# Two row-wise projections back to back, and another place for the fetched rows' products on VectorE, in a hybrid decoder block

## The chip, the cores and the metric

The kernel runs on one core of one Trainium2 chip. The metric is the device time of one execution in microseconds (us). The engines that matter here are TensorE (PE in the rows, PEld its weight loads), VectorE (DVE), ScalarE (ACT), GpSimd (POOL) and SyncE (SP), which issues the plain DMAs.

## What is computed

One decoder block over 256 tokens of width 2048 in float32: a norm, a projection whose columns feed two attentions and two gates, an output projection, and then a mixer in which each token picks 128 of 16384 experts. Cut to what matters:

```python
h = rms_norm(x, g_mix)
z = h @ w_in
q_a, k_a, v_a, c_q, c_kv, k_r, gate_a, gate_b = split(z)      # c_q: 512 columns, c_kv + k_r: 320
...
q = rms_norm(c_q, g_cq) @ w_uq                                # MLA: latent rows, normed again
kv = rms_norm(c_kv, g_ckv) @ w_ukv
...
x = x + mixed @ w_o
# PEER: u, v are (16384, 2048); expert (tokens, 128) holds indices, gate their weights
a = einsum('cd,ced->ce', h2, u[expert])
w = gelu(a) * gate
x = x + einsum('ce,ced->cd', w, v[expert])
return rms_norm(x, g_final)
```

## The kernel before

Every weight comes as a float32 tile `raw` and is split in two parts, `whi` (rounded to TensorE's fp32r format, on ScalarE, L108) and `wlo` (the remainder, on VectorE, L112). Three matmuls per product then give float32 accuracy: high by high, low by high, high by low. `feed_hi` loads and splits one unit of weights; there are three buffers for `raw` and two each for `whi` and `wlo`, so that a unit's `whi` can only be written when TensorE has read the unit two before it.

**The front.** `nblock` (L159) multiplies rows of tokens by streamed weights. The first projection, `pss_cq` (512 columns, 16 steps of six matmuls), runs while x is still being loaded; `make_x` scales x by the norm's gain for it, called from `ahead_x`. The norm's own factor does not go into the matmuls: `r1c` (one number a token) is applied to the finished rows by `rows_out` (L338), and `r1` (the same, laid along the free axis) to transposed results. To get it, ScalarE squares the rows of x (L248, eight instructions), VectorE sums them, ScalarE takes a root (L171), VectorE finishes the reciprocal root (L172 to L176) and makes two diagonal tiles `dg` (L255), and TensorE multiplies ones by them (L256). In the code this whole chain stands between `pss_cq` and the second row-wise projection, `rows_proj(320, ckr)` (L376). Then come the norms of the two latents (`norm_rows`), their transposes through TensorE (`tp`, L386 to L391), a rotary part `kro` that needs `sin` and `cos`, and the projection of kT (L146 and L151).

Up to the experts a scheduler sets each engine's order from the code; from L945 on the order is that of the code.

**The first expert sweep** (L948 to L1007) has 128 units. In unit j TensorE multiplies 16 high tiles (L952) and then 16 low tiles (L981) of `u` by the tokens' transposes, for 192 of the 256 tokens; in some units eight small matmuls (L958) that build a gate grid `G` stand between. VectorE multiplies earlier results (L962), adds two halves of the last unit's result (`add`, L905), and subtracts to make `wlo` of unit j+1 (`ready_lo`, L977); products with a finished grid follow (L979), and a comparison for a later grid (L940).

The other 64 tokens' experts are fetched row by row. `gathered()` is a generator with 130 steps: a step asks GpSimd for the next indirect DMA of 128 rows (L828) into one of two `urow` buffers and multiplies the previous one on VectorE by the tokens (L852, which also sums). The request for row i+1 writes the buffer that product i-1 has read, so GpSimd waits for that product. `gather_to(goal)` advances it; 54 steps (GU) belong to this sweep, spread evenly from the unit JR on (52 here), the rest to the second sweep (L1036), which multiplies by `v`.

Of the kernel before, what the change touches and what calls it, by code (L numbers as in the profile page):

```python
# [8 lines left out]
F32 = mybir.dt.float32  # L9
# [3 lines left out]
AF = mybir.ActivationFunctionType  # L13
OP = mybir.AluOpType
AX = mybir.AxisListType
PSUM = bass.MemoryType.PSUM

P = 128
D = 2048
KO = D // P  # L20
# [3 lines left out]
NJ = 128  # L24
# [19 lines left out]
class Work:  # L44
# [6 lines left out]
    def add(self, gen):  # L51
        self.gens.append(gen)
# [13 lines left out]
def block(tc, a, out):  # L66
    nc = tc.nc
    vec, act, pe, pool, sync = nc.vector, nc.scalar, nc.tensor, nc.gpsimd, nc.sync
# [89 lines left out]

    def nblock(pss, nk, act_c, ahead=None):  # L159
        for k in range(nk):  # L160
            if ahead and k % 4 == 0:
                ahead(k // 4)
            wh, wl = next(wts)
            for c, ps in enumerate(pss):
                cs = slice(c * P, (c + 1) * P)
                pe.matmul(ps, act_c[:, k, 0, cs], wh, start=k == 0, stop=False)  # L166
                pe.matmul(ps, act_c[:, k, 0, cs], wl, start=False, stop=False)  # L167
                pe.matmul(ps, act_c[:, k, 1, cs], wh, start=False, stop=k == nk - 1)  # L168
# [19 lines left out]
    def acc_tile():  # L188
        accs[0] += 1
        return ps_acc.tile([P, 512], F32, name="acc", bufs=4)  # L190
# [3 lines left out]
    xc = xp.tile([P, KO, 2, T], F32R, name="xc")  # L194
# [8 lines left out]
    def load_x(k0, k1):  # L203
        sync.dma_start(xT[:, k0:k1, :], a["xT"][:, k0:k1, :])

    def make_x(k0, k1):
        for k in range(k0, k1):
            act.activation(xc[:, k, 0], xT[:, k], AF.Copy, scale=gm[:, k:k + 1])
            vec.scalar_tensor_tensor(xc[:, k, 1], xT[:, k], gm[:, k:k + 1], xc[:, k, 0].bitcast(F32),
                                     op0=OP.mult, op1=OP.subtract)  # L210


    xn = s0.tile([P, 2, D], F32, name="xn")
    sp4 = s0.tile([P, 2, 4], F32, name="sp4")
    ss = s0.tile([P, 2], F32, name="ss")
    tmp1 = s0.tile([P, 2], F32, name="tmp1")

    def ahead_x(q):
        if q == 0:
            return  # L220
        if q < 3:
            make_x(4 * q + 4, 4 * q + 8)


    idle = s0.tile([P, 512], mybir.dt.bfloat16, name="idle")
# [1 line left out]
    ps = acc_tile()  # L227
# [6 lines left out]
    make_x(2, 4)  # L234
    feed_hi()()
    load_x(4, 8)
    make_x(4, 8)
    feed_hi()()
    load_x(8, 12)
    load_x(12, 16)  # L240
    pss_cq = [acc_tile() for _ in range(2)]
    nblock(pss_cq, KO, xc, ahead=ahead_x)
    for c in range(2):
        sync.dma_start(xn[:, c], a["x_rows"][c])
    for c in range(2):
        for i in range(4):
            d = slice(i * 512, (i + 1) * 512)
            act.activation(xn[:, c, d], xn[:, c, d], AF.Square, accum_out=sp4[:, c, i:i + 1])  # L248
    vec.tensor_reduce(ss, sp4, axis=AX.X, op=OP.add)
    vec.tensor_scalar(ss, ss, 1.0 / D, EPS, op0=OP.mult, op1=OP.add)  # L250
    rsqrt(r1c, ss, tmp1)
    dg = s0.tile([P, 2, P], F32, name="dg")
    ps = acc_tile()
    for c in range(2):
        vec.tensor_scalar(dg[:, c], ident, r1c[:, c:c + 1], None, op0=OP.mult)  # L255
        pe.matmul(ps[:, c * P:(c + 1) * P], ones, dg[:, c], start=True, stop=True)  # L256
    act.activation(r1, ps[:, :T], AF.Copy)
    st.close()


# [57 lines left out]
    ckr = tp_.tile([P, 2, 320], F32, name="ckr")  # L318
# [17 lines left out]
    def rows_out(dst, pss, cols):  # L336
        for c in range(2):
            act.activation(dst[:, c], pss[c][:, :cols], AF.Copy, scale=r1c[:, c:c + 1])  # L338

    def rows_proj(cols, dst):  # L340
        pss = [acc_tile() for _ in range(2)]
        nblock([p[:, :cols] for p in pss], KO, xc)
        rows_out(dst, pss, cols)
# [29 lines left out]
                                     op0=OP.mult, op1=OP.mult)  # L373

    rows_out(cq, pss_cq, 512)
    rows_proj(320, ckr)  # L376
    norm_rows(cq, 512, gcq)
    norm_rows(ckr, 256, gckv)
    for c in range(2):
# [262 lines left out]
    for b in range(KO):  # L642
        ps = acc_tile()
# [160 lines left out]
    for hp in range(16):  # L804
        ps = acc_tile()
# [76 lines left out]
    JR = None  # L882
    GU = 54
# [3 lines left out]
    def gather_to(goal):  # L887
        nonlocal gdone
        while gdone < STEPS and gdone <= goal:
            next(gat, None)  # L890
            gdone += 1
# [56 lines left out]
    for j in range(NJ):  # L948
        ps = acc_tile()
        ws = ready.pop(0)  # L950
        for k, (wh, wl) in enumerate(ws):
            pe.matmul(ps[:, :2 * TD], wh, hc[:, k].rearrange("p a t -> p (a t)"), start=k == 0, stop=False)  # L952
        fresh = []
        if hot and hot[0][0] + 2 <= j:
            G = ps_g.tile([P, 4, P], F32, name="G", bufs=2)
            _, o1, o2 = hot.pop(0)
            for q in range(4):
                pe.matmul(G[:, q], o1[:, q], o2[:, q], start=True, stop=True)  # L958
            fresh.append(G)
        while prods:  # L960
            bj, ge = prods.pop(0)
            vec.tensor_tensor(bj, bj, ge, op=OP.mult)  # L962
        add = evict(*last) if last else None
        ready_lo = feed_hi()
        old = gelus[:]
        gelus.clear()
        if add:
            add()
        work.pull(1.5)
        if JR is not None:  # L970
            gather_to((j - JR) * GU / (NJ - JR))
        rest = []
        while grids:
            rest += finish_gates(grids.pop(0))
        for g in old:
            finish_unit(*g)
        ready_lo()  # L977
        for bh, gv in rest:
            vec.tensor_tensor(bh, bh, gv, op=OP.mult)  # L979
        for k, (wh, wl) in enumerate(ws):  # L980
            pe.matmul(ps[:, :TD], wl, hc[:, k, 0], start=False, stop=k == KO - 1)  # L981
        last = (j, ps)
        grids += fresh
        if j == 0:
            scores(*behind)
            work.add(routing())
            qs.close()
            xs.close()
            b1 = bs.enter_context(tc.tile_pool(name="b1", bufs=1))
            B.append(b1.tile([P, NJ // 2, TD], F32, name="B0"))  # L990
        if JR is None and not work.gens:
            JR = j
            rt.close()
            b2 = bs.enter_context(tc.tile_pool(name="b2", bufs=1))
            B.append(b2.tile([P, NJ // 2, TD], F32, name="B1"))
            ps_g = hs.enter_context(tc.tile_pool(name="ps_g", bufs=1, space=PSUM))
        if JR is None:
            continue
        if groups < NG and groups * (NJ - 8 - JR) < (j + 1 - JR) * NG:
            hot.append((j, *one_hots(4 * groups)))  # L1000
            groups += 1
        if j == NJ - 2:
            assert not grids
            assert done == TD and not hot
            gs.close()
            wcp = bs.enter_context(tc.tile_pool(name="wcp", bufs=1, reuse_waits="tile"))
            wcs = [take_w(0)]  # L1007
# [28 lines left out]
    for n in range(NJ - 2):  # L1036
# [4 lines left out]
        if 80 <= n < 104 and n % 2 == 0:  # L1041
            c, i = divmod(n // 2 - 40, 4)
            d = slice(i * 512, (i + 1) * 512)
# [3 lines left out]
        for i in range(4):  # L1047
            i = (i + accs[0]) % 4
            d = slice(i * 512, (i + 1) * 512)
# [24 lines left out]
    for i in range(4):  # L1074
        d = slice(i * 512, (i + 1) * 512)
# [28 lines left out]
    for i in range(4):  # L1104
        d = slice(i * 512, (i + 1) * 512)
# [3 lines left out]
    for i in range(2):  # L1109
        d = slice(i * 512, (i + 1) * 512)  # L1110
# [3 lines left out]
    for i in range(2, 4):  # L1114
        d = slice(i * 512, (i + 1) * 512)
# [93 lines left out]
```

## Time and profile before

| | us |
|---|---|
| median of 3 runs | 1904.34 (1901.85 to 1908.06) |
| the profiled execution, whole | 1913.5 |
| its span, first to last instruction | 1911.7 |
| TensorE busy | 1870.5 (98%) |
| VectorE busy | 1593.1 (83%) |
| ScalarE busy | 1139.8 (60%) |

The profiled execution is one run, with the profiler on. Busy time of TensorE counts overlapping matmuls whole and is no measure of how fast it works; what it waited for is the better view.

### The profile page before, as it was taken

The page shows a single profiled execution, that of the slowest core. Times are in us where ns is not written, and L with a number is a line of the kernel's source. Part 1 is how long each engine was busy: PE and PEld are TensorE (multiplying, and loading weights), DVE is VectorE, ACT ScalarE, POOL GpSimd, SP SyncE. Part 2 cuts the span into 40 slices and gives each one's busy share as a digit, 9 for nine tenths or more (in the row PEclk, how much of TensorE's full clock was granted, in tenths as well). Part 3 has the DMA queues.
Part 4 walks back from the last instruction along what each step waited for, and adds up shares of the span by engine and source line. Part 5 has one row for each costly group of instructions (what it writes and reads, how often), then busy time and mean ns, then how long its engine had stood idle before and what let it go on. Part 6 is the DMA issues. An engine that isn't in the chain of part 4 may idle for free.

```text
span 1911.7 us, 28123 instructions
## 1 busy us (share of the span) xinstructions
PE 1870.5 (98%) x10874; PEld 1680.9 (88%) x10874; DVE 1593.1 (83%) x2277; ACT 1139.8 (60%) x1754; POOL 349.9 (18%) x192
## 2 busy tenths in 40 slices
PE   8999999999999999999999999999999999999996
PEld 6888888888888999999999999998788788887885
DVE  5768878658679799998899999998888898888887
ACT  7655766545555455555999998855444444444444
POOL 0000000000000000515243334333322123112210
PEclk9999999999999999999999999999999999999998
DMA  7554444455555566667798898889999999999983
GB/s 275 191 174 151 143 162 141 160 192 180 207 203 185 176 216 231 227 229 274 295 346 345 345 350 338 324 335 356 373 374 359 386 385 364 387 395 381 399 328 127
DMA packets 77910, 526.16 MB, mean 275 GB/s; under 512 B 9168, under 2 KB 11472, under 8 KB 15568
## 3 DMA queue, kind: packets, MB, share of 16 engines
q1 hardware_dynamic: 59344, 390.14, 56.6%
q0 software_dynamic: 18432, 134.23, 17.3%
q8 instruction: 85, 1.39, 0.3%
q14 instruction: 49, 0.40, 0.1%
HBM read 520.14 MB, written 4.19 MB: 274 GB/s over the span
## 4 chain that ended last, share of the span: by engine, by line
PE 60%; issue 16%; POOL 8%; DVE 6%; DMA 5%; ACT 5%; SPq 0%; POOLq 0%; DVEq 0%; ACTq 0%
PE acc L146 15%; PE o L1033 8%; PE acc L952 8%; POOL urow L828 8%; PE acc L151 7%; PE acc L981 5%; PE o L1050 4%; DMA raw<-v 4%; PE o L1052 4%; PE o L1051 4%; DVE wlo L112 3%; ACT whi L108 3%; PE acc L167 1%; PE acc L168 1%; PE acc L166 1%
## 5 line engine op out<-in xcount | busy, mean ns | idle before, releaser
L112 DVE TENSOR_TENSOR wlo<-raw,whi 128x2048 fp32r<-128x2048 f32 (+2 forms) x363 | 827.0, 2279 | 216.4 <-ACT whi L108 212.7
L108 ACT ACTIVATE whi<-raw 128x2048 fp32r<-128x2048 f32 (+2 forms) x363 | 688.6, 1897 | 450.3 <-DMA raw<-v 238.9
L952 PE MATMUL acc<-hc,whi 128*128 128x384 f32 x2048 | 382.8, 339 | 0.0
L952 PEld LDWEIGHTS acc<-hc,whi 128*128 128x128 f32 x2048 | 353.2, 189 | 0.0
L981 PE MATMUL acc<-hc,wlo 128*128 128x192 f32 x2048 | 252.9, 275 | 4.8 <-DVE wlo L112 4.8
L1033 PE MATMUL o<-wlo,wc 128*128 128x512 f32 x1020 | 252.5, 390 | 1.5 <-DVE wlo L112 1.5
L981 PEld LDWEIGHTS acc<-hc,wlo 128*128 128x128 f32 x2048 | 244.8, 193 | 6.3 <-DVE wlo L112 6.3
L1033 PEld LDWEIGHTS o<-wlo,wc 128*128 128x128 f32 x1020 | 191.0, 188 | 42.6 <-DVE wlo L112 2.9
L146 PE MATMUL acc<-xc,whi 128*128 128x512 f32 x928 | 227.6, 394 | 0.0
L828 POOL DMA_INDIRECT urow<-u_rows,iv x64 | 167.0, 2610 | 314.1 <-DVE urow L852 311.1
L1050 PE MATMUL o<-whi,wc 128*128 128x512 f32 x504 | 197.5, 392 | 4.3 <-ACT whi L108 3.8
L146 PEld LDWEIGHTS acc<-xc,whi 128*128 128x128 f32 x928 | 170.3, 189 | 32.1
L1051 PE MATMUL o<-whi,wc 128*128 128x512 f32 x504 | 196.2, 389 | 0.0
L1052 PE MATMUL o<-whi,wc 128*128 128x512 f32 x504 | 196.2, 389 | 0.0
L828 POOL DMA_INDIRECT vrow<-v_rows,iv x64 | 116.1, 1814 | 347.3 <-DVE h_nat L865 317.3
L852 DVE SCALAR_TENSOR_TENSOR urow<-urow,h_nat 128x2048 f32<-128x2048 f32 x64 | 146.2, 2285 | 21.9 <-DMA urow<-u_rows,iv 21.9
L865 DVE SCALAR_TENSOR_TENSOR h_nat<-vrow,gg,h_nat 128x2048 f32<-128x2048 f32 x63 | 147.8, 2346 | 0.0
L721 POOL TENSOR_TENSOR cand<-tv 128x256 f32<-128x256 f32 x16 | 14.0, 891 | 730.4 <-DVE tv L714 633.4
L902 ACT ACTIVATE ge<-acc 128x192 f32<-128x192 f32 x128 | 41.4, 324 | 152.7 <-PE acc L981 150.4
L151 PEld LDWEIGHTS acc<-xc,wlo 128*128 128x128 f32 x928 | 119.2, 191 | 4.5
L151 PE MATMUL acc<-xc,wlo 128*128 128x256 f32 x928 | 121.2, 283 | 0.0
L1050 PEld LDWEIGHTS o<-whi,wc 128*128 128x128 f32 x504 | 94.6, 188 | 28.5 <-ACT whi L108 8.3
(329 smaller groups left out, 2254.8 us busy)
## 6 DMA issues: line engine op xcount, KB each, us to landing
raw<-u SPq DMA_DIRECT2D x128, 1024.0 KB, 5.1
raw<-v SPq DMA_DIRECT2D x128, 1024.0 KB, 8.2
raw<-w_ga SPq DMA_DIRECT2D x16, 1024.0 KB, 4.8
raw<-w_gb SPq DMA_DIRECT2D x16, 1024.0 KB, 4.8
raw<-w_o SPq DMA_DIRECT2D x16, 1024.0 KB, 4.9
raw<-w_pq SPq DMA_DIRECT2D x16, 1024.0 KB, 4.9
raw<-w_q SPq DMA_DIRECT2D x8, 1024.0 KB, 4.8
raw<-w_a SPq DMA_DIRECT2D x8, 1024.0 KB, 4.9
```

The costliest lines, as they stand in the source:

```text
L108: act.activation(hi, raw, AF.Copy)
L112: vec.tensor_tensor(lo, raw, hi.bitcast(F32), op=OP.subtract)
L146: pe.matmul(ps, ws[k][0], act_c[:, k].rearrange("p a t -> p (a t)"), start=k == 0, stop=False)
L151: pe.matmul(ps[:, :T], ws[k][1], act_c[:, k, 0], start=False, stop=k == nk - 1)
L828: pool.indirect_dma_start(out=dst, out_offset=None, in_=table, in_offset=bass.IndirectOffsetOnAxis(ap=idx, axis=0))
L865: later(vec.scalar_tensor_tensor(h_nat, r, gg[:, i:i + 1], h_nat, op0=OP.mult, op1=OP.add))
L952: pe.matmul(ps[:, :2 * TD], wh, hc[:, k].rearrange("p a t -> p (a t)"), start=k == 0, stop=False)
L981: pe.matmul(ps[:, :TD], wl, hc[:, k, 0], start=False, stop=k == KO - 1)
L1033: pe.matmul(O[c][i], st_, v[:, i * 512:(i + 1) * 512], start=first and k == 0, stop=last and k == len(ss) - 1)
L1050: pe.matmul(O[0][i], S[0], vh[:, d], start=n == 0, stop=False)
L1051: pe.matmul(O[0][i], S[1], vh[:, d], start=False, stop=False)
L1052: pe.matmul(O[1][i], S[2], vh[:, d], start=n == 0, stop=False)
```

## The change

Four edits:

1. `ahead_x` is called at every step of the first projection, makes one tile of x six steps ahead, and only tiles 4 and 5 (instead of 4 to 7) are made before the projection begins.
2. The second row-wise projection, `pss_ck`, comes directly after the first. The squares are called from inside it (ahead of steps 4 and 8), and the sum, the root, `dg` and the multiplication by ones after it. The latter's result has a PSUM tile of its own, in a pool that is closed at once; `acc_tile` is called once less.
3. `rows_proj(320, ckr)` becomes `rows_out(ckr, pss_ck, 320)`.
4. In the first expert sweep `gather_to` is called after `ready_lo` and the grid's products instead of before them, and its goal is spread over one unit less: the last unit makes no step.

```diff
     def nblock(pss, nk, act_c, ahead=None):
         for k in range(nk):
-            if ahead and k % 4 == 0:
-                ahead(k // 4)
+            if ahead:
+                ahead(k)
...
-    def ahead_x(q):
-        if q == 0:
-            return
-        if q < 3:
-            make_x(4 * q + 4, 4 * q + 8)
+    def ahead_x(k):
+        if k + 6 < KO:
+            make_x(k + 6, k + 7)
+
+    def squares_x(c):
+        for i in range(4):
+            d = slice(i * 512, (i + 1) * 512)
+            act.activation(xn[:, c, d], xn[:, c, d], AF.Square, accum_out=sp4[:, c, i:i + 1])
...
-    make_x(4, 8)
+    make_x(4, 6)
...
-    for c in range(2):
-        for i in range(4):
-            d = slice(i * 512, (i + 1) * 512)
-            act.activation(xn[:, c, d], xn[:, c, d], AF.Square, accum_out=sp4[:, c, i:i + 1])
+    pss_ck = [acc_tile() for _ in range(2)]
+    psn = ExitStack()
+    ps_n = psn.enter_context(tc.tile_pool(name="ps_n", bufs=1, space=PSUM))
+    nblock([p[:, :320] for p in pss_ck], KO, xc, ahead=lambda k: squares_x(k // 4 - 1) if k in (4, 8) else None)
     vec.tensor_reduce(ss, sp4, axis=AX.X, op=OP.add)
...
-    ps = acc_tile()
+    ps = ps_n.tile([P, 512], F32, name="nacc")
...
+    psn.close()
...
-    rows_proj(320, ckr)
+    rows_out(ckr, pss_ck, 320)
...
         work.pull(1.5)
-        if JR is not None:
-            gather_to((j - JR) * GU / (NJ - JR))
...
             vec.tensor_tensor(bh, bh, gv, op=OP.mult)
+        if JR is not None and j < NJ - 1:
+            gather_to((j - JR) * GU / (NJ - 1 - JR))
```

What this makes of the engines' orders is shown at three places. On ScalarE and VectorE the order of x's tiles and the first weights is the same before and after. The line numbers of the changed kernel are a few higher.

ScalarE around the norm, before (`xn` are the squares, `tmp` the root, `whi` with 1280 columns the units of the 320-column projection):

```order
L248 ACTIVATE xn,sp_99<-xn 128x512 x6
L289 ACTIVATE dist<-dist 128x384
L171 ACT_TABLE_LOAD
L171 ACTIVATE tmp_101<-ss 128x2
L338 ACTIVATE cq<-acc,r1c 128x512 x2
L257 ACTIVATE r_93<-acc 128x256
L108 ACTIVATE whi<-raw 128x1280
```

ScalarE around the norm, after:

```order
L225 ACTIVATE xn,sp_99<-xn 128x512 x6
L108 ACTIVATE whi<-raw 128x1280
L171 ACT_TABLE_LOAD
L171 ACTIVATE tmp_101<-ss 128x2
L343 ACTIVATE cq<-acc,r1c 128x512
L108 ACTIVATE whi<-raw 128x1280
L294 ACTIVATE dist<-dist 128x384
L343 ACTIVATE cq<-acc,r1c 128x512
L371 ACTIVATE njunk,nmean<-cq 128x512 x2
L108 ACTIVATE whi<-raw 128x1280
```

The second unit of the 320-column projection is now split ahead of the root, and the third and fourth between the norm's later steps.

ScalarE where `sin` and `cos` are made, before, while the 320-column projection ran:

```order
L311 ACTIVATE turns<-ang 128x64
L313 ACT_TABLE_LOAD
L313 ACTIVATE sin<-ang 128x64
L366 ACTIVATE njunk,nmean<-cq 128x512
L314 ACTIVATE cos<-turns 128x64
L108 ACTIVATE whi<-raw 128x1280
```

ScalarE there, after (`whi` with 2048 columns is the second unit of kT's weights):

```order
L371 ACTIVATE njunk,nmean<-ckr 128x256
L316 ACTIVATE turns<-ang 128x64
L318 ACT_TABLE_LOAD
L318 ACTIVATE sin<-ang 128x64
L319 ACTIVATE cos<-turns 128x64
L171 ACT_TABLE_LOAD
L171 ACTIVATE nt<-nmean 128x2
L139 ACTIVATE cqT<-tp 128x4x128
L108 ACTIVATE whi<-raw 128x2048
```

`sin` and `cos` with their two table loads have moved behind the 320-column projection, into the time of kT's first unit. TensorE's order at that place, after (`tp` from `ckr` and `kro` are the transposes that need the second latent's norm and the rotary part):

```order
L260 MATMUL nacc<-dg,ones 128x128 x2
L146 MATMUL acc<-xc,whi 128x512 x4
L391 MATMUL tp<-ident,cq 128x128 x4
L146 MATMUL acc<-xc,whi 128x512 x12
L151 MATMUL acc<-xc,wlo 128x256 x16
L395 MATMUL tp<-ident,ckr 128x128 x2
L396 MATMUL tp<-ident,kro 128x128
```

Before, the first transposes of `ckr` stood five low matmuls into kT's second unit; now they stand right behind kT's first.

VectorE in a unit with a product late in the first expert sweep, before:

```order
L962 TENSOR_TENSOR B_9359<-B_9359,ge 128x192
L905 TENSOR_TENSOR ge<-acc,ge 128x192
L852 SCALAR_TENSOR_TENSOR urow,dots<-urow,h_nat 128x2048
L112 TENSOR_TENSOR wlo<-raw,whi 128x2048
L962 TENSOR_TENSOR B_9359<-B_9359,ge 128x192
```

VectorE there, after:

```order
L967 TENSOR_TENSOR B_9363<-B_9363,ge 128x192
L910 TENSOR_TENSOR ge<-acc,ge 128x192
L112 TENSOR_TENSOR wlo<-raw,whi 128x2048
L857 SCALAR_TENSOR_TENSOR urow,dots<-urow,h_nat 128x2048
L967 TENSOR_TENSOR B_9363<-B_9363,ge 128x192
```

The product with the fetched rows has changed places with the subtraction. Runs of three such units in a row, which stand nine times in the order before, stand eleven times in the order after, the last of them in units 121 to 123 (before: 119 to 121).

## Rows read from the trace of the kernel before

**Rows 1.** TensorE's waits: what was waited for, us in total, times, longest

```profile
PE acc L981 <- DVE wlo L112: 4.8, 3, 2.5
```

**Rows 2.** TensorE's timeline, front: start us, us, instruction, [idle before <-releaser]

```profile
31.85 0.39 PE L168 MATMUL acc<-whi,xc 128*128 128x512 f32 x1
35.22 1.22 PE L256 MATMUL acc<-dg,ones 128*128 128x128 f32 x4 [2.98 <-DVE dg L255]
...
42.00 0.31 PE L166 MATMUL acc<-whi,xc 128*128 128x320 f32 x1
...
48.90 0.31 PE L168 MATMUL acc<-whi,xc 128*128 128x320 f32 x1
...
53.00 3.82 PE L146 MATMUL acc<-xc,whi 128*128 128x512 f32 x16
...
58.57 3.82 PE L146 MATMUL acc<-xc,whi 128*128 128x512 f32 x16
...
105.52 0.76 PE L146 MATMUL acc<-ckvT,whi 128*128 128x512 f32 x2 [2.08 <-DVE qnT L427]
```

**Rows 3.** Stretches: us, busy us (instructions) by engine, granted clock, DMA share, GB/s

```profile
36.00:38.00 2.00, 2.00 (x10) 2.00 (x9) 0.44 (x3) 1.66 (x4) 0.95 (x3) 0.50 0.19 72
...
106.00:108.00 2.00, 2.00 (x9) 1.77 (x8) 0.89 (x3) 0.39 (x1) 0.00 (x0) 0.52 0.91 254
```

**Rows 4.** ScalarE's timeline, front

```profile
26.84 1.27 ACT L108 ACTIVATE whi<-raw 128x1280 fp32r<-128x1280 f32 x1 [0.94 <-PE acc L168]
...
32.22 1.28 ACT L171 ACT_TABLE_LOAD   x1
33.52 0.20 ACT L171 ACTIVATE tmp<-ss 128x2 f32<-128x2 f32 x1
34.87 1.27 ACT L338 ACTIVATE cq<-acc,r1c 128x512 f32<-128x512 f32 x2 [1.15 <-DVE r1c L176]
```

**Rows 5.** VectorE's timeline, front

```profile
28.14 1.50 DVE L112 TENSOR_TENSOR wlo<-raw,whi 128x1280 fp32r<-128x1280 f32 x1 [3.17 <-ACT whi L108]
...
53.40 0.68 DVE L140 TENSOR_TENSOR cqT<-tp,cqT 128x512 fp32r<-128x512 f32 x1
54.00 0.18 DVE L355 TENSOR_TENSOR ropem<-ckr,cos 128x32 f32<-128x32 f32 x1
...
55.66 0.20 DVE L383 COPY kro<-kro 128x64 f32<-128x64 f32 x1
```

**Rows 6.** TensorE's timeline, first expert sweep

```profile
1238.60 2.03 PE L981 MATMUL acc<-hc,wlo 128*128 128x192 f32 x16 [1.51 <-DVE wlo L112]
...
1271.52 2.98 PE L952 MATMUL acc<-hc,whi 128*128 128x384 f32 x16
1277.05 3.73 PE L981 MATMUL acc<-hc,wlo 128*128 128x192 f32 x16 [2.55 <-DVE wlo L112]
...
1284.81 1.93 PE L981 MATMUL acc<-hc,wlo 128*128 128x192 f32 x16
...
1289.39 1.93 PE L981 MATMUL acc<-hc,wlo 128*128 128x192 f32 x16
```

**Rows 7.** VectorE's timeline, the three units ahead of the longest of those waits

```profile
1259.11 2.29 DVE L852 SCALAR_TENSOR_TENSOR urow<-urow,h_nat 128x2048 f32<-128x2048 f32 x1
...
1261.31 2.29 DVE L112 TENSOR_TENSOR wlo<-raw,whi 128x2048 fp32r<-128x2048 f32 x1
...
1272.48 2.29 DVE L852 SCALAR_TENSOR_TENSOR urow<-urow,h_nat 128x2048 f32<-128x2048 f32 x1 [2.79 <-DMA urow<-u_rows,iv]
```

**Rows 8.** GpSimd's requests, one in each sweep

```profile
1261.67 2.75 POOL L828 DMA_INDIRECT urow<-u_rows,iv  x1 [7.34 <-DVE urow L852]
...
1428.42 1.08 POOL L828 DMA_INDIRECT vrow<-v_rows,iv  x1 [5.01 <-DVE h_nat L865]
```

**Rows 9.** VectorE's timeline around the second of them

```profile
1428.27 0.42 DVE L876 TENSOR_TENSOR wc<-B,wc 128x256 fp32r<-128x256 f32 x1
1428.61 2.29 DVE L112 TENSOR_TENSOR wlo<-raw,whi 128x2048 fp32r<-128x2048 f32 x1
```

## The prediction

> **What bounds the kernel now.** I read the list of TensorE's waits first. TensorE is busy in 98% of the span, so a change of order can win only what TensorE waits for, and what a slow clock costs behind a wait. Of the waits that the change can touch, three stand out: the one for `dg` in the front, three for `wlo` in the first expert sweep, 4.8 us together [rows 1], and none else. Then I read TensorE's timeline at both places, and after it the engines that were late.
>
> In the front, the last matmul of the 512-column projection starts at 31.85, and the next instruction, the multiplication by ones, at 35.22 after 2.98 us of idling [rows 2]. What follows is slow: the stretch from 36 to 38 has a granted clock of 0.50, which is the lower of the two levels, 1.2 GHz [rows 3]. From 42.00 to 48.90 the 320-column matmuls come every 0.147 us (47 steps in 6.90 us) [rows 2], and the 24 between the ones and 42.00 at the same pace would take 3.5 us. With some 0.45 us for the ones at full clock that makes 4.0, while 35.22 to 42.00 took 6.78. So the clock cost 2.8 us behind a wait of 2.98, and the place costs 5.8 us in all.
>
> In the sweep, the last and longest wait is 2.55 us ahead of 1277.05. From there to the next unit's low half at 1284.81 it takes 7.76 us, where a unit without a wait takes 4.58 (1284.81 to 1289.39) [rows 6]: 3.2 us of slow clock on top. The wait of 1.51 at 1238.60 was not followed by it: its sixteen low matmuls took 2.03 us, not 3.73 [rows 6]. With the smallest of the three (4.8 less 2.55 and 1.51, or 0.74) the three places cost 8.0 us. Why TensorE waited is on VectorE's timeline. The product that started at 1272.48 had idled 2.79 us for its fetched row [rows 7], and `wlo` of the next unit stands behind it in the order. It is the third product in three units; GpSimd requests a row 0.36 us after the product two before has ended at 1261.31, at 1261.67, and the request alone takes 2.75 us [rows 7, 8].
>
> **The change part by part.** The finer `make_x` leaves ScalarE's and VectorE's order of x's tiles and first weights as it was, so it moves nothing: 0.
>
> The second projection now stands directly behind the first, and the ones behind it. The 5.8 us above go, if the projection's weights are split in time. Its first two units are: ScalarE split one at 26.84 already [rows 4]. The third's high part has to wait for a buffer until TensorE has read the first (24 matmuls from 32.1, so 35.6). With 1.27 us for `whi` and 1.50 for `wlo` [rows 4, 5], and the root's steps and `dist` between, I get 39.55, and TensorE wants it at 39.3: a wait of 0.3. So 5.5 us are gained by the end of kT's first unit, which would come at 53.1 instead of 58.57 [rows 2]. The norm itself hides: its root, `dg` and ones have the 14 us of the projection, and nothing asks for them sooner. If that cover were gone, the 2.98 us would be back.
>
> Here something new comes due. The transposes of `ckr` and `kro`, which stood five low matmuls into kT's second unit, now stand behind kT's first, and `sin`, `cos` and the second root lie ahead of them. In the new order the chain is: kT's first `wlo` on VectorE, which I have end at 48.5 by running the order by hand with the durations of before; two short steps on the angles, to 48.9; a table load and `sin`, 1.30 us from load to activation (32.22 to 33.52) [rows 4], and `cos`, to 50.6; the rotary steps on VectorE, 1.86 us (54.00 to 55.86) [rows 5], to 52.5, while ScalarE loads the other table and takes the root; from root to use 1.35 us before (33.52 to 34.87) [rows 4], of which, with a transposed copy of 0.68 [rows 5] in it too, some 2.0 are left: 54.5. TensorE is free at 53.1 and waits 1.4 us. Bounds: 0 if VectorE is ahead of my hand run, and 2.98, as much as the wait removed. I take 1.4, so the front gains **4.1 us** (5.5 less 1.4). Whether the clock falls behind it: it did behind 2.98 and 2.08 us (0.52 from 106 to 108) [rows 2, 3] and did not behind 1.51 [rows 6]; 1.4 is nearest to the last, so I count nothing. If it falls as it did behind `dg`, 2.8 come off, and 1.3 stay.
>
> What one table switch costs is weighed here. The row has the next activation 1.30 us behind the start of the load [rows 4]. The Trainium skill, "ScalarE: Activation LUTs", section "What ACT_TABLE_LOAD costs", gives 1283 ns for the load and 1380 ns more for a drain, 2.66 us a switch. By it the two loads on this chain would make the wait about 2.8 us longer and eat two thirds of the front's gain. No drain shows behind the load in this trace, so the row decides.
>
> In the sweep, `wlo` no longer stands behind the product. A late row then delays the product, and `wlo` of the unit after only when the product is late by more than VectorE's slack. I ran the triple ahead of 1277.05 by hand in the new order: `wlo` from 1259.11 to 1261.3, product to 1263.52, `wlo` from 1264.05, product to 1269.1, `wlo` to 1271.9 (TensorE asks at 1274.33, so the 2.55 us are gone), third product when its row lands, next `wlo` behind it, asked for at 1278.9. When does the row land? Before, it landed at 1272.45 after a request from 1261.67 that took 2.75 us. Now the product ends at 1263.52, so 2.21 us later, at 1274.7, if the request takes as long; the next `wlo` is then done at 1279.7, 0.8 too late. But GpSimd's request does not always take 2.75: one in the second sweep took 1.08 [rows 8]. At 1261.67 VectorE had just begun the 2.29 us of `wlo` [rows 7]; at 1428.42 it ran a short multiplication, and `wlo` began only at 1428.61 [rows 9]. In the new order the product is the unit's last step and short steps come behind it, so 1.08 is the nearer row: the row lands at 1273.0, and `wlo` is 0.85 early. The last of the eleven triples stands in units 121 to 123, where the units without a grid are shortest, and there I leave a wait of 1.0 without a slow clock. The sweep gains **7.0 us** (8.0 less 1.0). Bounds: 8.0, and, with requests of 2.75, waits of 0.8 at the late triples, 2.4 us or less.
>
> [...]
>
> **What this is of the median.** The profiled execution took 1913.5 us, 9.2 more than the median of 1904.34. The front's waits hang on instruction order in every run, so I carry them over whole. The sweep's waits hang on when a fetched row lands. Runs that are 9 us shorter likely have fewer or shorter ones, the clock's 3.2 us among them; I take half of the 7.0, so 3.6 (rounded up). Against the profiled time the sum is 1913.5 less 11.1, or 1902.4; against the median, 1904.34 less 4.1 and 3.6, or **1896.5** (rounded).
>
> **The rivals.** First, only the front pays. The fetched rows come no earlier, the waits for `wlo` just move a unit on, or they are hardly there without the profiler: 1904.34 less 4.1, about 1900. For it: the sweep's price rests on one place with a slow clock. Against it: the 2.79 us of VectorE's idling show plainly what blocks `wlo`.
>
> Second, the new wait for the transposes brings the lower clock: the front keeps 1.3 and the sweep pays 3.6, about 1899.5. For it: 1.4 is close to 2.08. Against it: 1.51 passed.
>
> Third, slower. The request starts 0.36 us after the product, `wlo` some 0.53 us after it (two short steps of 0.27). If the request hasn't yet done its writing by then, GpSimd is held until `wlo` ends, and the request ends half a us later after the product than it does today, while the product itself already comes 2.2 us later in its unit. Then each of eleven triples stalls TensorE by about 1.0 us (0.8 for late landing and 0.2 to 0.5 more), and the last with the clock, 4.8: some 15.8 us against today's 8.0, so 7.8 worse, and with the front's 4.1 about **1908**. It decides from the point at which a request ends more than 2.75 us after its start. For it: the margin is 0.2 us. Against it: in units with a comparison (L940) a third short step stands ahead of `wlo`.
>
> Fourth, everything is paid in full, no new wait and the sweep's whole 8.0: about 1891. That the change doesn't do what it says holds for `make_x` alone, at 0.
>
> **How the numbers follow.** The forecast, both pay: 0.62. Only the front: 0.22. The front's clock falls: 0.08. Slower: 0.04. Paid in full: 0.04. The range goes from 1890.0, a full payment and 1 us of scatter below it, to 1902.5, the front alone with its new wait at 2.98 (1901.8) and as much scatter. About 0.3%, 5.7 us, is what a measurement of this kernel can tell from no change, so faster means below 1898.6: most of the forecast's case and the full payment, with a little of the rest, 0.68. Slower is above 1910.0, which the third rival reaches if a second late triple meets the slow clock; I leave it the whole 0.04. The rest, 0.28, is within.
>
> **What would show it.** In the profile after, the ones should start at about 47 without a wait ahead of them, and the stretch from 36 to 38 should have a granted clock of 1.00. TensorE should wait 1 to 2 us ahead of the transposes of `ckr`, and kT's second unit should start near 54.5. In the sweep the waits for `wlo` should be at most one of about 1 us, and requests of GpSimd behind a product near 1.1 us. Requests of 2.75 there, or waits of 1 us in every triple, would make the third rival right. A wait of over 2 us in the front with a clock of 0.5 behind it would make the second right. A front as predicted and a total near 1900 would leave the first.

## The result, and the profile after

| | us |
|---|---|
| kernel before, median of 6 runs | 1905.76 (1901.85 to 1910.38) |
| changed kernel, median of 6 runs | 1896.20 (1892.05 to 1898.81) |
| ratio of the runs, with its 95% interval | 0.9933 (0.9915 to 0.9951) |
| the profiled execution after, whole, and its span | 1898.81, 1897.0 |

The changed kernel is faster by 9.6 us between the medians. The ratio of the runs is not that of the two medians: by it the gain is 12.8 us (9.3 to 16.2), so at least 0.49%. The forecast was 1896.5 (1890.0 to 1902.5), by the case in which front and sweep both pay.

TensorE's waits after, of which the page of before had `dg` with 2.98 us and `wlo` with 4.8 [rows 1, 2] (columns as there):

```profile
PE o L1055 <- DVE ge L910: 2.8, 1, 2.8
PE o L1055 <- ACT whi L108: 2.2, 4, 1.0
PE acc L146 <- DVE qnT L432: 2.1, 1, 2.1
...
PE tp L395 <- DVE ckr L377: 0.7, 1, 0.7
PE acc L986 <- DVE wlo L112: 0.7, 1, 0.7
```

The wait for `dg` is gone, and the three for `wlo`, in units 108, 115 and 122, are one of 0.72 (at 1116.95, in unit 93). New are one of 0.73 ahead of the transposes of `ckr`, which was forecast, and one of 2.80 for `ge`, which was not.

TensorE's timeline in the front, after; these rows answer to [rows 2]:

```profile
32.10 0.39 PE L168 MATMUL acc<-whi,xc 128*128 128x512 f32 x1
32.33 0.30 PE L166 MATMUL acc<-whi,xc 128*128 128x320 f32 x1
...
46.77 0.61 PE L260 MATMUL nacc<-dg,ones 128*128 128x128 f32 x4
...
51.47 2.07 PE L151 MATMUL acc<-xc,wlo 128*128 128x256 f32 x16
54.27 0.44 PE L395 MATMUL tp<-ident,ckr 128*128 128x128 f32 x2 [0.73 <-DVE ckr L377]
...
55.01 3.21 PE L146 MATMUL acc<-xc,whi 128*128 128x512 f32 x13
...
61.13 0.40 PE L166 MATMUL acc<-whi,xc 128*128 128x256 f32 x2
```

The 320-column projection starts 0.23 us behind the last matmul of the other. From there to the ones it takes 14.4 us, and nothing waits ahead of the ones. The granted clock, which was 0.50 from 36 to 38 [rows 3], is 1.00 there now, and 0.58 in another place, where the second sweep begins:

```profile
36.00:38.00 2.00, 2.00 (x16) 2.00 (x15) 1.58 (x8) 1.66 (x2) 0.00 (x0) 1.00 0.85 201
1295.00:1299.00 4.00, 4.00 (x12) 3.11 (x12) 2.78 (x5) 2.29 (x3) 0.00 (x0) 0.58 0.94 320
```

VectorE's timeline near the end of the first sweep, after, in place of [rows 7]:

```profile
1269.86 2.28 DVE L857 SCALAR_TENSOR_TENSOR urow<-urow,h_nat 128x2048 f32<-128x2048 f32 x1
...
1272.07 0.35 DVE L967 TENSOR_TENSOR B<-B,ge 128x192 f32<-128x192 f32 x1
1272.34 0.35 DVE L910 TENSOR_TENSOR ge<-acc,ge 128x192 f32<-128x192 f32 x1
1272.61 2.28 DVE L112 TENSOR_TENSOR wlo<-raw,whi 128x2048 fp32r<-128x2048 f32 x1
1275.34 2.29 DVE L857 SCALAR_TENSOR_TENSOR urow<-urow,h_nat 128x2048 f32<-128x2048 f32 x1 [0.46 <-DMA urow<-u_rows,iv]
```

GpSimd's request behind the first of these products:

```profile
1272.42 0.94 POOL L833 DMA_INDIRECT urow<-u_rows,iv  x1 [4.01 <-DVE B L967]
```

It starts as long after the product as before (0.35 us, with the product taken to end where the next instruction starts), now 0.19 ahead of `wlo`, and takes 0.94 where it took 2.75 [rows 8]. The shortest, median and longest of all 64 requests for rows of `u`, the last nine of which fall behind this sweep, are, before and after, in ns:

```profile
L828 POOL DMA_INDIRECT urow<-u_rows,iv x64: 1081/2745/2750, 892.3 to 1370.5; - x64
```

```profile
L833 POOL DMA_INDIRECT urow<-u_rows,iv x64: 936/1145/2868, 887.4 to 1357.5; - x64
```

Of the 55 in the sweep itself, 54 took more than 2.6 us before; after, only one does (2.65, the second of all), and the 2868 ns belong to the second sweep.

### Where the time went

This table is made from TensorE's timeline of each kernel's profile, in us. *Front* runs from the start of the first projection's last 512-column matmul to the first matmul of `va`, the row-wise projection behind kT (32.10 to 61.13 after); *middle* from there to the first matmul of the first expert sweep; *sweep* from there to the start of the last unit's low half; *turn* from there to the second sweep's first matmul; *second* from there to its last one.

| profile | front | middle | sweep | turn | second |
|---|---|---|---|---|---|
| before | 33.31 | 599.8 | 638.2 | 1.77 | 590.2 |
| before_look1 | 34.18 | 599.8 | 639.7 | 1.76 | 589.4 |
| before_look2 | 33.84 | 598.3 | 634.4 | 1.76 | 588.7 |
| after | 29.03 | 598.9 | 630.0 | 4.73 | 585.7 |
| after_beside | 29.05 | 598.8 | 629.1 | 4.65 | 586.7 |
| front_only | 29.03 | 597.3 | 637.6 | 5.34 | 585.6 |
| product_last | 33.40 | 599.9 | 628.6 | 1.76 | 582.8 |
| one_step_between | 30.59 | 598.5 | 639.0 | 1.77 | 586.3 |
| late_wlo | 29.04 | 597.3 | 628.9 | 2.79 | 586.9 |
| early_angles | 28.38 | 599.8 | 629.4 | 4.22 | 582.7 |
| both_mended | 28.38 | 598.4 | 629.3 | 2.78 | 589.3 |
| bank_turn | 29.03 | 597.3 | 628.8 | 1.76 | 583.7 |
| bank_turn_early_angles | 28.41 | 599.9 | 629.4 | 1.77 | 593.4 |
| bank_turn_beside | 29.03 | 598.7 | 628.7 | 1.76 | 590.4 |

Between the two first profiles the front gave 4.3 us and the sweep 8.2, and the turn took 3.0. Kernels that have the front's edits take 28.4 to 29.1 us there, and those with the product last take 628.6 to 630.0 for the sweep; without these edits the times are longer and vary more. The second sweep lies anywhere between 583 and 593, with no order by kernel.

### The profile page after: what moved, and what is told of

Same layout as the page of the kernel before. It is cut to its first block, busy times and chain, and to the rows that moved or that the text cites. A ratio compares the mean times of both kernels' runs of the same rounds, so it can differ in the third digit from the quotient of the medians.

```text
span 1897.0 us, 28115 instructions
## 1 busy us (share of the span) xinstructions
PE 1862.9 (98%) x10874; PEld 1677.5 (88%) x10874; DVE 1592.6 (84%) x2277; ACT 1139.6 (60%) x1754; POOL 272.6 (14%) x192
## 4 chain that ended last, share of the span: by engine, by line
PE 82%; DVE 7%; ACT 5%; DMA 4%; issue 2%; SPq 0%; DVEq 0%; ACTq 0%
PE acc L957 16%; PE acc L146 15%; PE o L1038 11%; PE acc L986 10%; PE acc L151 8%; PE o L1055 5%; PE o L1056 5%; PE o L1057 5%; DVE wlo L112 4%; ACT whi L108 3%; DMA raw<-v 2%; PE G L963 2%; PE acc L167 1%; PE acc L168 1%; PE acc L166 1%
## 5 line engine op out<-in xcount | busy, mean ns | idle before, releaser
L833 POOL DMA_INDIRECT vrow<-v_rows,iv x64 | 126.0, 1969 | 340.7 <-DVE h_nat L870 314.5
L833 POOL DMA_INDIRECT urow<-u_rows,iv x64 | 78.4, 1225 | 394.6 <-DVE urow L857 271.3
```

Of the source, the lines that this page charges most:

```text
L833: pool.indirect_dma_start(out=dst, out_offset=None, in_=table, in_offset=bass.IndirectOffsetOnAxis(ap=idx, axis=0))
```

## The experiments

### The two parts apart

front_only has the front's edits alone: the call of `gather_to` is back where it was.

```diff
         work.pull(1.5)
+        if JR is not None:
+            gather_to((j - JR) * GU / (NJ - JR))
...
-        if JR is not None and j < NJ - 1:
-            gather_to((j - JR) * GU / (NJ - 1 - JR))
```

> The front's edits alone; the product of the fetched rows stays ahead of the subtraction. If the prediction's terms hold and add up, this gains 4.1 us over before (ratio about 0.9978), TensorE's first matmul of va starts near 61.1 (65.16 before), and the first expert sweep still waits for wlo some 4.8 us with requests of 2.75 us. If the sweep's waits are only there under the profiler and the front pays everything, it gains about 9 us (ratio 0.995).

Measured: 1902.78 beside 1907.05, ratio 0.9977 (0.9963 to 0.9991), so 4.4 us (1.7 to 7.1). Its front is that of the changed kernel to the hundredth, 29.03. The waits for `wlo` are still there, in other sizes:

```profile
PE acc L986 <- DVE wlo L112: 3.9, 3, 1.4
PE o L1055 <- DVE ge L910: 3.4, 1, 3.4
```

They come to 3.9 us, and the granted clock is 1.00 through the whole sweep, which all the same takes 637.6, or 7.6 us more than after. Another 1.4 us are waits of the grid's matmuls for VectorE; the rest is in no list of waits. So the waits for `wlo` are not all that a late request costs.

product_last has the other part alone: the call moved as in the changed kernel, the front as before.

> The place of the products alone; the front as before. If the prediction's sweep term holds, 3.6 us less than before in the timed runs (0.998) and 7 us less in the profiled sweep, with requests near 1.1 us, at most one wait for wlo of about 0.7 us, and a wait of 2 to 3 us at the start of the second sweep. If the two parts must add up to the measured 9.6 us, then 5 to 5.5 (0.997). If the sweep's waits are only the profiler's, nothing (1.000).

Measured: 1900.87 beside the same 1907.05, ratio 0.9972 (0.9959 to 0.9986), so 5.3 us (2.7 to 7.8). The list of waits has none for `wlo` in the first sweep any more, and `dg` with 3.0 as before. The two parts come to 9.7 by the ratios and to 10.5 between the medians (4.3 and 6.2), the whole change to 12.8 and 9.6: within intervals this wide they add up. That the front pays everything, or that the sweep's waits are the profiler's, is out: both intervals exclude zero. The wait of 2 to 3 us at the turn, which was expected here, did not come (1.76): it belongs to the front's part, not to this one.

### A quarter of a microsecond between product and subtraction

one_step_between is product_last with one difference: the product changes places with one short multiplication of the next unit. Products and subtractions keep their order among themselves; only one short step, not two or three, lies between a product and the next `wlo`. Against the kernel before:

```diff
         while prods:
             bj, ge = prods.pop(0)
             vec.tensor_tensor(bj, bj, ge, op=OP.mult)
+        if JR is not None and j > JR + 1:
+            gather_to((j - 1 - JR) * GU / (NJ - 1 - JR))
         add = evict(*last) if last else None
...
         work.pull(1.5)
-        if JR is not None:
-            gather_to((j - JR) * GU / (NJ - JR))
```

> Beside product_last, one short multiplication (L962, 0.27 us) changes places with the product, so that one short step instead of two or three stands between a product and the next subtraction; order of subtractions and products among themselves is the same. If what counts is whether GpSimd's request gets in ahead of the subtraction, the subtraction now begins 0.27 us behind the product and the request 0.36 us behind it: requests take about 2.8 to 3.0 us again, the waits for wlo come back, and the time is that of before (1.000) or up to 7.8 us more (1.004). If only the order of product and subtraction counts, it is like product_last (0.997 to 0.998), with requests still near 1.1 us or without effect of their length.

Measured: 1909.21, ratio 1.0014 (1.0001 to 1.0027), so 2.7 us slower than before (0.2 to 5.1) and 8 slower than product_last. GpSimd's 64 requests there, as above shortest, median and longest in ns:

```profile
L828 POOL DMA_INDIRECT urow<-u_rows,iv x64: 935/3012/3016, 888.3 to 1366.5; - x64
```

Two of them in GpSimd's timeline:

```profile
1271.32 3.01 POOL L828 DMA_INDIRECT urow<-u_rows,iv  x1 [5.91 <-DVE ge L905]
1277.07 3.01 POOL L828 DMA_INDIRECT urow<-u_rows,iv  x1 [2.73 <-DVE ge L905]
```

and VectorE beside them:

```profile
1270.97 0.35 DVE L905 TENSOR_TENSOR ge<-acc,ge 128x192 f32<-128x192 f32 x1
1271.24 2.27 DVE L112 TENSOR_TENSOR wlo<-raw,whi 128x2048 fp32r<-128x2048 f32 x1
...
1276.98 2.28 DVE L112 TENSOR_TENSOR wlo<-raw,whi 128x2048 fp32r<-128x2048 f32 x1
1279.18 0.35 DVE L962 TENSOR_TENSOR B<-B,ge 128x192 f32<-128x192 f32 x1
1283.83 2.29 DVE L852 SCALAR_TENSOR_TENSOR urow<-urow,h_nat 128x2048 f32<-128x2048 f32 x1 [4.29 <-DMA urow<-u_rows,iv]
```

The request at 1271.32 comes 0.08 us behind the start of `wlo` and ends at 1274.33, some 0.82 behind `wlo`'s end; in the changed kernel the one at 1272.42 came 0.19 ahead of `wlo` and was done in 0.94, most of it while `wlo` ran. So in this sweep it is the start that decides, within less than 0.1 us: 47 of the requests here start 0.08 us behind `wlo` and take 3.0, while in the changed kernel even one that starts 0.01 behind it takes 0.94. What GpSimd still has to do once it is held is nearly the whole request. The product at 1283.83 then waits 4.29 us for its row, and TensorE behind it, in the last of three waits for `wlo` that come to 5.8 us, and the granted clock is 0.50 from 1289 to 1293:

```profile
1288.65 3.73 PE L981 MATMUL acc<-hc,wlo 128*128 128x192 f32 x16 [4.48 <-DVE wlo L112]
```

This is the mechanism of the prediction's third rival. The Trainium skill ("SBUF — State Buffer", "SBUF: two separate sides") says that a VectorE instruction with two inputs in SBUF and a GpSimd instruction that reads SBUF take a shared pair of ports from each other: whichever starts first has it for its whole length, and the other is held. The trace agrees where `wlo` starts first (3.01). Where the request does, it shows no holding: sixteen `wlo` of the changed kernel's first sweep that began within 0.6 us behind a request's start took 2.27 to 2.31 us, as much as those with no request near. (Ten `wlo` earlier in that sweep that met a TENSOR_TENSOR of GpSimd did take longer, 2.49 to 2.83.)

### The new wait ahead of the transposes

early_angles writes the angles' loads and steps ahead of the distances, so that ScalarE makes `sin` and `cos` before kT's first unit, and the transposes of `ckr` stand in kT's second unit again.

```diff
+    posc_i = tp_.tile([P, 2], I32, name="posc_i")
+    sync.dma_start(posc_i, a["pos_col"])
+    invf = tp_.tile([P, 32], F32, name="invf")
+    sync.dma_start(invf, a["invf"].to_broadcast([P, 32]))
     sync.dma_start(gf, a["g_ffn"])
...
-    posr = tp_.tile([P, T], F32, name="posr")
-    vec.tensor_copy(posr, posr_i)
     posc = tp_.tile([P, 2], F32, name="posc")
     vec.tensor_copy(posc, posc_i)
-    dist = sp_.tile([P, 384], F32, name="dist")
...
     act.activation(cos, turns, AF.Sin)
 
+    posr = tp_.tile([P, T], F32, name="posr")
+    vec.tensor_copy(posr, posr_i)
+    dist = sp_.tile([P, 384], F32, name="dist")
...
```

> The changed kernel with the angles' loads and steps written earlier, so that sin and cos with their table load come ahead of kT's first unit and the transposes of ckr and kro stand in kT's second unit again. If the new wait of 0.73 us ahead of the transposes is all that this place costs, va starts 0.7 us sooner after the first projection's end than the 29.0 us of the changed kernel, and the time is that of the changed kernel within its scatter (0.993). If ScalarE's table loads now delay the norm or the weights, a wait of 1 us or more comes up in the 320-column projection or kT instead.

Measured: 1894.83 beside 1908.83, ratio 0.9934 (0.9913 to 0.9955). The front takes 28.38 where it took 29.03, 0.65 less, and no wait ahead of these transposes is left. In the timed runs that is too small to tell.

### The wait where the second sweep begins

TensorE's timeline of the changed kernel at the turn:

```profile
1290.00 1.93 PE L986 MATMUL acc<-hc,wlo 128*128 128x192 f32 x16
1294.73 0.50 PE L1055 MATMUL o<-whi,wc 128*128 128x512 f32 x1 [2.80 <-DVE ge L910]
...
1296.30 0.63 PE L1057 MATMUL o<-whi,wc 128*128 128x512 f32 x1
```

The second sweep's first matmul waits for VectorE's last addition of two halves, and its matmuls take 0.63 us in place of 0.39 for a while, at the lower clock shown above. The first twelve last from 1294.73 to 1299.18, or 4.45 us. First theory: that addition is late, since a subtraction for the second sweep stands ahead of it. late_wlo puts that subtraction behind it.

```diff
-        ready_lo()
+        if j < NJ - 1:
+            ready_lo()
...
     evict(*last)()
+    ready_lo()
```

> The changed kernel with one thing more: the last unit of the first sweep makes its subtraction (for the second sweep's first unit) behind the last addition of two halves and not ahead of it. In the changed kernel TensorE waits 2.80 us there for that addition. If the subtraction in front of it is the cause, 2.2 us of that wait go, 2.2 us off the changed kernel (about 0.992 of before), and the second sweep's first low half waits 0.3 us at most. If the addition is late for another reason, nothing changes (0.9933).

Measured: 1894.86 beside 1907.05, ratio 0.9928 (0.9912 to 0.9945). The wait is 0.86 and the turn 2.79 in place of 4.73, so 1.94 us of the 2.2 expected are gone; and the clock stays at 1.00, so that the same twelve matmuls take 2.89. The timed gain cannot be told from the changed kernel's.

both_mended is early_angles and late_wlo in one kernel.

> The changed kernel with the angles early and the last unit's subtraction behind the last addition (early_angles and late_wlo together). If the waits of 0.73 and 2.80 us are separate, 2.7 us less than the changed kernel: about 0.992 of before, with neither wait in the trace. If the second sweep's first unit is late instead, no more than early_angles alone.

Measured: 1898.84 beside 1908.83, ratio 0.9955 (0.9938 to 0.9972). Front and turn are as short as in the two single kernels (28.38 and 2.78), and yet it is no faster than either: its second sweep took 589.3 us.

Why is the turn 1.76 in all kernels with the front of before, product_last too? There the second sweep ran six matmuls before it waited, here in product_last:

```profile
1295.42 0.41 PE L1050 MATMUL o<-whi,wc 128*128 128x512 f32 x1
...
1297.37 0.50 PE L1050 MATMUL o<-whi,wc 128*128 128x512 f32 x1 [0.41 <-DVE ge L905]
```

In the built programs the last four units of the first sweep keep their sums in PSUM banks 0, 1, 2, 3 before and 2, 3, 1, 0 after, and the second sweep starts with bank 1 before and bank 0 after: after, its first accumulator is the very bank that is freed last. The front's edit brought this about: it takes one tile less from the rotation of four (the ones' result has a pool of its own). That did more than shift it by one, which would have moved the last unit's bank and the second sweep's first one together: the order in which the banks come round in the sweep has changed too. bank_turn begins the second sweep two accumulators further on.

```diff
+    accs[0] += 2
     fs = ExitStack()
```

> The changed kernel, and the second sweep begins with other two of its four accumulators. In the changed kernel its first matmul waits 2.80 us for the last addition of the first sweep, and the clock is low for some 3 us behind it; in kernels with the front of before, the first six matmuls run and the seventh waits 0.4. The program of the changed kernel has the last unit's sums in PSUM bank 0, which is the second sweep's first accumulator; that of before has them in bank 3, its third. If the one tile that the front takes less has shifted the banks and that is the wait's cause, the second sweep's first matmul starts some 2.4 us sooner behind the last low half, the seventh matmul waits 1.4 us at most, and the time is 2.5 to 4 us below the changed kernel (0.991 to 0.992 of before). If VectorE's lateness is the cause whatever the bank, nothing changes (0.9933).

Measured: 1897.82 beside 1906.93, ratio 0.9954 (0.9939 to 0.9969). The trace did what was expected: no wait at the first matmul, 1.0 at the seventh, no slow clock.

```profile
1286.99 1.93 PE L986 MATMUL acc<-hc,wlo 128*128 128x192 f32 x16
1288.75 0.41 PE L1056 MATMUL o<-whi,wc 128*128 128x512 f32 x1
...
1291.32 0.50 PE L1056 MATMUL o<-whi,wc 128*128 128x512 f32 x1 [1.02 <-DVE ge L910]
```

The time, expected at 0.991 to 0.992, did not follow. Nor did it with the early angles:

> bank_turn and early_angles together: 0.7 us less than bank_turn if the two waits are independent, about 0.991 of before; like bank_turn within the scatter if not.

Measured: 1897.56, ratio 0.9947 (0.9927 to 0.9966); its second sweep took 593.4. So the changed kernel and bank_turn ran side by side once more.

> The changed kernel again, on the same chip as bank_turn_beside. 0.9933 of before again; in the trace 629 to 630 us from the first sweep's first matmul to its last low half, and 4 to 5 us from there to the second sweep's first matmul.

Measured: 1897.27 beside 1908.96, ratio 0.9945 (0.9927 to 0.9962).

> bank_turn once more, beside the changed kernel on one chip. bank_turn's trace had the first matmul of the second sweep 1.8 us behind the last low half and not 4.7, but its timed runs gave 0.9954 of before, where the changed kernel had 0.9933. If the 3 us are on the path that sets the end, it is 2 to 3 us below after_beside. If the second sweep is held by something else and gives them back, the two agree within 1 us, and the trace shows a second sweep that is longer by about as much.

Measured: 1896.18, ratio 0.9929 (0.9911 to 0.9947). It lies under after_beside by 1.1 us between the medians and by 3.1 by the ratios, inside both intervals, so that neither nothing nor the expected 2 to 3 us is excluded. In the profiles the turn is 2.9 shorter and the second sweep 3.7 longer. The stretch from 1300 to 1860, first of after_beside and then of bank_turn_beside:

```profile
1300.00:1860.00 560.00, 557.46 (x2450) 458.84 (x2449) 475.87 (x333) 261.28 (x186) 138.59 (x73) 1.00 0.96 373
```

```profile
1300.00:1860.00 560.00, 553.64 (x2429) 454.37 (x2428) 474.42 (x330) 259.98 (x184) 138.36 (x73) 1.00 0.96 372
```

Both have the DMA engines busy for 96% and move the same 372 to 373 GB/s, and bank_turn_beside waits longer for `whi` (5.6 us in all against 2.5). That fits a second sweep whose pace is set by the weights' transfers, in which a start 3 us sooner is waited off later. It was not shown by taking the transfers away, and with a second sweep that scatters by 10 us, these runs cannot exclude a gain of 3 us either.

What this scatter is made of, the profiles do show. TensorE's waits within the second sweep come to 1.3 us in its two shortest (early_angles and product_last) and to 5.0 to 6.9 us in its five longest. In these five most of the waiting is for `whi`, and ScalarE, which makes it, mostly waited for a weight tile that was still being fetched. The line for `whi` of early_angles and that of bank_turn_early_angles, the longest:

```profile
PE o L1054 <- ACT whi L108: 1.3, 2, 0.9
```

```profile
PE o L1055 <- ACT whi L108: 4.2, 4, 2.9
```

Which executions have late tiles, and why, is open.

### The kernel before, profiled twice more

> The kernel before once more, for its trace alone. The prediction counted 2.8 us of slow clock behind the wait for dg, and 3.2 behind a wait of 2.55 us for wlo, from one profiled execution. If a wait of that length is always followed by the lower clock, the stretch from 36 to 38 shows 0.50 again and the place costs 5.8 us. If it depends on the execution, it shows 1.00 as in one_step_between, and the place costs about 3 us. The sweep's waits for wlo: 4.8 us again if they are fixed by the order, other places and sums (0 to 5) if they hang on when rows land.

> The same as before_look1, a further execution: the granted clock from 36 to 38, and how long TensorE waits for wlo in the first sweep.

Measured: 1915.63 and 1907.69, one run each. The wait for `dg` took 3.7 and 4.9 us (2.98 in the first profile), and the lower clock came behind both. The waits for `wlo` in before_look1:

```profile
PE acc L981 <- DVE wlo L112: 7.8, 4, 4.1
```

and in before_look2:

```profile
PE acc L981 <- DVE wlo L112: 4.1, 4, 1.3
```

In before_look1 the longest, 4.12 us, was followed by the lower clock again, in before_look2 (longest 1.34) none was. The sweep took 639.7 and 634.4 us.

## Why the prediction was right, and where it was not

**The front.** 5.5 us were forecast by the end of kT's first unit and 4.1 after the new wait. In the profiles kT's first unit ended 26.7 us behind the last 512-column matmul before (58.57 less 31.85) and some 21.4 after (54.27 less the wait of 0.73 less 32.10), so 5.3; and the front as a whole gave 4.3. The wait of 0.3 for the third unit is there with 0.25 us (39.37 to 39.77, where 0.15 is the pace). The wait ahead of the transposes is 0.73 and not 1.4: by hand the chain ended at 54.5, on the chip at 54.27 in an execution that lies 0.25 us later from the start, so the hand was half a us slow; and TensorE arrived 0.2 later than thought. Both table loads were followed by the next activation 1.30 and 1.29 us behind their start (48.84 to 50.14, and 50.56 to 51.85), as the row of before had it; no drain of the length that the Trainium skill gives ("ScalarE: Activation LUTs", "What ACT_TABLE_LOAD costs": 1.38 us a switch) shows, and by it the wait would have been 3.5 us (an estimate, 0.73 and twice 1.38). The clock stayed at 1.00, so the second rival did not come.

**The term of the clock in the front** was counted as if it always came: 2.8 us behind the wait for `dg`. It came in four of the five profiles with the old front. In one_step_between the same wait, 2.99 us, was followed by 1.00, and the front took 30.59, not 33.3. The front less that wait is 27.6 us in one_step_between, 29.0 in before_look2 and 30.3 to 30.4 in the other three. So the place cost 3 us or more of waiting in all five, and of slow clock nothing once, 1.4 once and 2.8 three times.

**The sweep.** The mechanism was right: GpSimd's request ahead of `wlo`, 0.94 to 1.15 us where it took 2.75, and rows that come in time. The size was not so good. The term was 7.0 in the profile, with 1.0 left in units 121 to 123; measured are 8.2 between the two profiles, with no wait in those units. For the timed runs I halved the term, because they are shorter than the profiled one. product_last gives 5.3 us (2.7 to 7.8), an interval that holds the 3.6 as well as the 7.0. Against the halving speak the profiles: four of the five profiles in which the request meets `wlo` took 637.6 to 639.7 (634.4 the fifth), against 628.6 to 630.0 in all nine others. So the loss is there in each execution; what varies is its size and whether the clock falls. And by front_only it is not made of the waits for `wlo` and the slow clock alone, from which the 8.0 was added up.

**The turn** was missing altogether. That one tile less is taken from the accumulators stood in my own list of what the change does, and I gave it no price. In the profile it cost 3.0 us of waiting, and the slow clock behind that another 1.6 (4.45 less 2.89), which the table has in the second sweep. How much of it reaches the end is open (above): front_only, with a turn of 5.34 in its profile, still gained 4.4.

**The total** is closer than its terms. 7.7 us of gain were forecast and 9.6 measured between the medians, or 12.8 by the ratio; the sweep's term was too small by 1.7 (3.6 against 5.3) and the turn had none. That the time itself came within 0.3 us is luck in part: three more runs of the kernel before raised its median by 1.4, from 1904.34 to 1905.76, which made up for most of the gain that was not forecast.

**The slower rival** gave its mechanism and its point: a request that starts just behind `wlo` takes over 2.75. In one_step_between it took 3.01, and cost 8 us against the kernel with the request ahead; against before it is 2.7 us and not the 7.8 that I had, since only two of the triples stalled by more than 0.2 us (1.17 and 4.48), and not each of eleven.

## What to carry to other kernels

Where GpSimd asks for rows beside a wide two-input instruction of VectorE, look at which of the two starts first: 0.27 us of order decided here about 8 us of time, and short steps between the product that frees the buffer and the next wide instruction are the place for the request. A pool that gives out one tile more or less can change a rotation for the rest of the kernel; look where the rotation ends, not only where the tile was taken. And a gain ahead of a stage whose transfers are busy for 96% is to be measured behind that stage.

## What was not expected of the hardware

The clock behind a wait of the same length is not the same in each execution. The wait for `qnT`, 2.08 us, is in all fourteen profiles, with matmuls of the same shape behind it. In eight of them the granted clock is 0.50 to 0.59 in the third and fourth microsecond after it, in six it stays at 1.00. Of the three profiles of the kernel before, two have the lower clock there and before_look2 has not. It moves the stretch called *middle* by some 1.5 us (597.3 and 598.4 against 598.8 and 599.8; what parts each pair by 1 us was not looked for). A term for the clock behind a wait of 2 to 3 us is thus a chance and not a sum.

Also, the rule that the start decides does not hold in the second sweep: three requests of the changed kernel took 3.28 us there and one 5.48, though they had started 0.18 us or more ahead of `wlo`, like seventeen others that took 1.08. The profile of the kernel before has six of 3.28. What sets these apart is open.
